# Splitting weight pieces with two GpSimd-issued transfers and one ScalarE operation in a hybrid decoder block

## The chip, the cores and the metric

The kernel runs on one core of one Trainium2 chip. The metric is the device time of one execution in microseconds. Below, PE is the matrix engine, DVE is VectorE, ACT is ScalarE, POOL is GpSimd and SP is SyncE; SP, ACT and POOL can issue DMA transfers.

## The reference

For 512 tokens of 1024 channels, one decoder layer is computed:

```
u = rmsnorm(h);  P = u @ W_in            # combined projection, 8280 columns
A = gated delta rule over q, k, v (causal conv, chunks, 8 heads), gated norm
B = sparse attention: indexer picks top 128 causal keys per query, 8 heads
m = sigmoid(gate_A) * A + sigmoid(gate_B) * B
h = h + m @ W_out
h = h + (silu(conv(hn @ W_up_gate)) * conv(hn @ W_up_val)) @ W_down
out = rmsnorm(h)
```

Everything is float32.

## The kernel before

The weights lie in DRAM as 139 **pieces** of 128 rows by 1024 values (512 KB each), in the order in which they are used (`_pack_weights`). A product with float32 accuracy is made of three passes in the format float32r (L201 to L203): each operand is held as a high part (the value rounded to float32r) and a low part (the rest), and low by high, high by low and high by high are summed in PSUM. The weights' parts are the tiles `whi` and `wlo`; the activations' parts are `xgh`/`xgl`, `uTh`/`uTl`, `mix`, `hTh`/`hTl` and `act`. A piece feeds 24 matmuls of 512 columns or 48 of 256.

`load` (L183) brings a piece from DRAM into the tile `raw` by a transfer on SP. `piece` (L191) then makes the parts: ACT rounds `raw` into `whi` (L193), and POOL or DVE subtracts, `wlo = raw - whi` (L194). The callers choose the engine: `token_major` and `channel_major` give the pieces of the mixers to POOL, except that the second piece of each pair in the second half of the delta rule goes to DVE (L494, L508, L546); the output projection (L832), the up projection from its third group on (L904) and the down projection (L950) give theirs to DVE. `raw`, `whi` and `wlo` have three buffers each, so up to three loaded and three split pieces wait ahead of PE. The first three pieces are split by halves in `split` (L229), which the change leaves alone.

The order of the work on each engine is found by the scheduler of the tile framework, which places instructions by a simulated timeline; a few pairs are ordered by hand (`after`). Around the pieces stand: the start (x, the value projection, the norm; L234 to L277), the decay and the indexer (L337 to L450, DVE chains `gd` and `iq`/`iqf`), the gated delta rule in two halves (`gdn_half`, L467), each with an inverse of 32x32 blocks on DVE (L571 to L579: tiles `wi`, `tw`), the top-128 search (L676 to L680), the attention (L696 to L729), the gates (L735 to L802), the output projection (L831), the up projection (L903) and the down projection (L943). POOL also makes `uTl` (L417), the masks `ge` (L522), scaled queries `qT` (L540) and the gate products (L764) between the pieces.

The lines that the change touches most:

```
def piece(lo_engine):
    raw, hi, lo = load()
    A.copy(hi, raw)
    lo_engine.tensor_sub(lo, raw, hi.bitcast(F))
    return hi, lo
```

Of the kernel before, what the change touches and what calls it, by code (L numbers as in the profile page):

```python
# [9 lines left out]
F = mybir.dt.float32  # L10
R = mybir.dt.float32r
I32 = mybir.dt.int32
AF = mybir.ActivationFunctionType
OP = mybir.AluOpType
# [4 lines left out]
D = 1024  # L19
# [22 lines left out]
def _in_chunks():  # L42
    """The projection's columns in the order in which the kernel takes them."""
    t = []
    t.append(("dv", [_DV, _DV + 128]))
    t.append(("small", None))
    t += [("iq", [_IQ + 256 * j, _IQ + 256 * j + 128]) for j in range(2)]
    gdn = [[("gdn", [_QKV + 1024 * part + 512 * hh + 256 * j + 128 * i for i in range(2)])
            for part in (1, 0, 2) for j in range(2)] for hh in range(2)]
    dsa = [("dk", [_DKV, _DKV + 128])]  # L50
    dsa += [("dq", [_DQ + 256 * j, _DQ + 256 * j + 128]) for j in range(4)]
    t += gdn[0] + dsa + gdn[1]
    off = {"z": _Z, "ga": _GA, "gb": _GB}
    t += [(k, [off[k] + 256 * j, off[k] + 256 * j + 128]) for k, j in _GATES]
    return t


def _pack_weights(w_in, w_out, w_up, w_down):
    """All weights as pieces of [128 rows, 1024 values], in the order of their use."""
    out = []  # L60

    def chunk(w, starts):
        c = np.concatenate([w[:, s:s + 128] for s in starts], axis=1)
        c = c.reshape(2, 4, 128, 256).transpose(0, 2, 1, 3).reshape(2, 128, 1024)
        out.extend([c[0], c[1]])

    for kind, starts in _in_chunks():
        if kind == "small":
            c = np.zeros((D, 128), w_in.dtype)
            c[:, 0:64] = w_in[:, _IK:_IK + 64]  # L70
            c[:, 64:80] = w_in[:, _A:_A + 16]
            c[:, 80:88] = w_in[:, _IW:_IW + 8]
            out.append(c.reshape(8, 128, 128).transpose(1, 0, 2).reshape(128, 1024))
        else:
            chunk(w_in, starts)
    for j in range(4):
        chunk(w_out, [256 * j, 256 * j + 128])
    for f in range(NF):
        chunk(w_up, [128 * f, FF + 128 * f])
    for half in range(2):  # L80
        c = w_down[:, 512 * half:512 * half + 512].reshape(NF // 2, 2, 128, 512)
        out.extend(c.transpose(0, 2, 1, 3).reshape(NF // 2, 128, 1024))
    return np.ascontiguousarray(np.stack(out))
# [3 lines left out]
def hybrid_block(ctx: ExitStack, tc: tile.TileContext, x: bass.AP, xc: bass.AP, wp: bass.AP,  # L87
# [22 lines left out]

# [1 line left out]
    ident = const.tile([128, 128], F, name="ident")  # L112
# [14 lines left out]
    def after(ins, before):  # L127
        """Keeps the order of two instructions of one engine."""
        tc.add_manual_dep(ins.ins, before.ins.name,
                          mybir.DependencyInfo(mybir.DependencyClass.NoSync, mybir.DependencyReason.DATA),  # L130
                          reason="order")
        return ins

    def rsqrt(y, v, tmp, it):
        """y = 1/sqrt(v) by Newton's steps from the bits' estimate."""
        V.tensor_scalar(it, v.bitcast(I32), -0.5, 1597463007.0, op0=OP.mult, op1=OP.add)
        cur = it.bitcast(F)
        for _ in range(3):
            V.scalar_tensor_tensor(tmp, cur, -0.5, cur, op0=OP.mult, op1=OP.mult)
            V.tensor_mul(tmp, tmp, v)  # L140
            V.scalar_tensor_tensor(y, tmp, 1.5, cur, op0=OP.add, op1=OP.mult)
            cur = y
# [13 lines left out]
    def part_of(ss, name, bufs, part=(eps, neps), eng=V):  # L156
        """ss/D + part, and -1/2 of it, of one value per partition."""
        p = const.tile([128, 2], F, name=name, bufs=bufs)
# [4 lines left out]
    def rms_of(ss, part=(eps, neps), out=None):  # L163
        """1/sqrt(ss/D + part) of one value per partition; a Newton step makes up for the table."""
        w = const.tile([128, 5], F, name="rms", bufs=4)
# [9 lines left out]
    def load_sqrt(after):  # L175
        """Brings in the square root's table once the value `after` is there."""
        A.activation(warm, after, AF.Sqrt, scale=0.0, bias=ones[:, 0:1])

# [1 line left out]
    pipe = ctx.enter_context(tc.tile_pool(name="pipe", bufs=1))  # L180
    pos = [0]

    def load():  # L183
        raw = pipe.tile([128, 1024], F, name="raw", bufs=3)
        nc.sync.dma_start(raw, wp[pos[0]])
        pos[0] += 1
        hi = pipe.tile([128, 1024], R, name="whi", bufs=3)
        lo = pipe.tile([128, 1024], R, name="wlo", bufs=3)
        return raw, hi, lo

    def piece(lo_engine):  # L191
        raw, hi, lo = load()
        A.copy(hi, raw)  # L193
        lo_engine.tensor_sub(lo, raw, hi.bitcast(F))  # L194
        return hi, lo

    def passes(o, lhs, rhs, first, last, shared=False):
        """o += lhs^T rhs with both operands in two parts. In a shared bank only the bank's first
        product carries the start, which clears the marks of the whole bank."""
        (lh, ll), (rh, rl) = lhs, rhs  # L200
# [9 lines left out]

# [1 line left out]
    wz = psum.tile([128, 512], F, name="wz", tag="rec", bufs=2)  # L212
# [77 lines left out]
    def token_major(eng):  # L290
        """One 256-column chunk: two banks, each with two token blocks [128, 2, 256]."""
        pcs = [piece(eng), piece(eng)]
# [19 lines left out]

# [1 line left out]
    PR = tc.alloc_tile_pool(name="PR", bufs=1, side="right", reuse_waits="tile")  # L314
# [6 lines left out]

# [1 line left out]
    dv = PR.tile([128, NT, 256], F, name="dv", tag="k4", bufs=2)  # L323
# [3 lines left out]

# [1 line left out]
    smT = PR.tile([128, 512], F, name="smT", tag="y", bufs=2)  # L329
# [6 lines left out]

# [1 line left out]
    def red(o, i, op=OP.add):  # L338
# [23 lines left out]

# [1 line left out]
    def sc8(name):  # L364
# [46 lines left out]

# [1 line left out]
    for k in range(KT):  # L413
# [3 lines left out]
        (V, P)[k % 2].tensor_sub(uTl[:, k], uv, uTh[:, k].bitcast(F))  # L417
# [1 line left out]
    iq = []  # L419
# [13 lines left out]

# [1 line left out]
    score = {}  # L435
# [15 lines left out]

# [1 line left out]
    def conv_silu(p, ti, dst=None):  # L453
# [13 lines left out]
    def gdn_half(hh):  # L467
# [23 lines left out]

        # keys
        for j in range(2):
# [11 lines left out]
        V.tensor_mul(kd, rk, kde[:, :, hs])  # L505
        # queries
        for j in range(2):
# [7 lines left out]

        # decayed products of keys with keys and queries
        for c in range(NT):
# [25 lines left out]

        # values
        for j in range(2):
# [8 lines left out]

        # inverses of the diagonal 32x32 blocks, one block per partition
        bl = dram.tile([64, 1024], F, name="bl%d" % hh)
# [23 lines left out]

        # merge the blocks: 32 -> 64 -> 128
        UT = PL.tile([128, 16, 64], F, name="UT", tag="g4", bufs=2)
# [32 lines left out]

        # the recurrence over chunks
        St = PL.tile([128, HH, 128], F, name="St", tag="St")
# [32 lines left out]

        # gated norm of the heads, up to the gate
        so = sc("so")
# [16 lines left out]

# [1 line left out]
    V.memset(mask[:, 0:128], 0.0)  # L671
# [9 lines left out]

# [1 line left out]
    dk = PR.tile([128, 2, 512], F, name="dk", tag="k4", bufs=2)  # L683
# [49 lines left out]

# [1 line left out]
    h_t = FL.tile([128, NT, D], F, name="h")  # L735
# [67 lines left out]

# [1 line left out]
    hTh = const.tile([128, KT, S], R, name="hTh", tag="uTh")  # L805
# [9 lines left out]
    def channels(tb, hn, order=None):  # L815
        """hn of one token block to channel-major parts; `order`: the product that goes before."""
        for q in range(2):
# [60 lines left out]

# [1 line left out]
    act = []  # L880
# [42 lines left out]

# [1 line left out]
    gf = FR.tile([128, D], F, name="gf")  # L925
# [102 lines left out]
```

## Time and profile before

| | us |
|---|---|
| three runs, median (lowest to highest) | 972.58 (971.25 to 973.08) |
| the profiled execution, first to last instruction (span) | 966.1 |
| busy: PE / DVE / ACT / POOL | 928.7 / 626.6 / 440.9 / 203.2 |
| splitting: ACT rounding, 136 pieces | 142.6 |
| splitting: subtraction on POOL, 60 pieces | 146.1 |
| splitting: subtraction on DVE, 76 pieces | 94.3 |

The profile gives the profiled execution's span alone; the median of the runs is 6.5 us above it, and that difference stands for what lies around the span. Busy time is time in which an engine has an instruction under way; a matmul's end is modelled, so a busy PE need not be at its best pace.

### The profile page before, as it was taken

Reading aid. Unit: us, or ns where it says so; the run is one execution under the profiler, and the core shown is the slowest. Engines: PE = TensorE matmul, PEld = TensorE weight load, DVE = VectorE, ACT = ScalarE, POOL = GpSimd, SP = SyncE. Lnnn points to the kernel's source line nnn. Section 1 sums busy time; section 2 is a strip of 40 time slices with the busy share of each in tenths; the row PEclk is TensorE's granted clock in tenths of the full one; section 3 lists DMA queues with packets and bytes.
Section 4 is the critical chain, followed back from the end, with each engine's and each line's share of the span. In section 5 each row is a group of like instructions: output and inputs, shape, how many; then the busy total and the mean of one; then the engine's idle time right before and its main releaser. Section 6 shows DMA issues by size and latency. Waiting matters only on the chain.

```text
span 966.1 us, 14640 instructions
## 1 busy us (share of the span) xinstructions
PE 928.7 (96%) x5671; PEld 801.9 (83%) x5671; DVE 626.6 (65%) x1262; ACT 440.9 (46%) x938; POOL 203.2 (21%) x116
## 2 busy tenths in 40 slices
PE   8979999998899899899999999999999999999997
PEld 8858887876787798799999999888888888888886
DVE  5897999997638969866663546655555655522424
ACT  7446674422367773245543436443434443422213
POOL 3734244412011263211244032000000000000201
PEclk9989999999999999999999999999999999999999
DMA  8222222323310131311323222332223223232222
GB/s 326 88 88 88 89 83 71 112 83 89 99 34 26 62 89 66 99 51 50 135 85 104 83 89 88 108 97 99 88 87 98 99 89 107 88 108 90 88 66 87
DMA packets 35381, 88.76 MB, mean 92 GB/s; under 512 B 11472, under 2 KB 12784, under 8 KB 35312
## 3 DMA queue, kind: packets, MB, share of 16 engines
q1 hardware_dynamic: 24048, 82.05, 25.7%
q10 hardware_dynamic: 11264, 5.79, 2.4%
q8 instruction: 44, 0.72, 0.3%
q14 instruction: 25, 0.20, 0.1%
HBM read 84.66 MB, written 3.16 MB: 91 GB/s over the span
## 4 chain that ended last, share of the span: by engine, by line
PE 72%; DVE 20%; ACT 3%; DMA 2%; issue 1%; ACTq 0%; POOL 0%; SPq 0%; DVEq 0%
PE acc L201 18%; PE acc L203 18%; PE acc L202 18%; DVE y L458 3%; PE d L202 3%; PE d L203 3%; PE d L201 3%; DVE tw L574 2%; DVE wi L576 2%; PE lg L700 1%; DVE mask L679 1%; PE lg L718 1%; DVE top L678 1%; DMA MT<-bl 1%; DVE mask L448 1%
## 5 line engine op out<-in xcount | busy, mean ns | idle before, releaser
L193 ACT CAST whi<-raw 128x1024 fp32r<-128x1024 f32 x136 | 142.6, 1049 | 175.7 <-PE acc L203 76.8
L194 POOL TENSOR_TENSOR wlo<-raw,whi 128x1024 fp32r<-128x1024 f32 x60 | 146.1, 2436 | 309.7 <-ACT whi L193 275.4
L194 DVE TENSOR_TENSOR wlo<-raw,whi 128x1024 fp32r<-128x1024 f32 x76 | 94.3, 1241 | 149.7 <-ACT whi L193 149.6
L202 PE MATMUL acc<-hTh,wlo 128*128 128x512 f32 (+1 forms) x368 | 141.8, 385 | 0.0
L201 PE MATMUL acc<-hTl,whi 128*128 128x512 f32 (+1 forms) x368 | 141.1, 386 | 0.3 <-DVE hTl L827 0.3
L203 PE MATMUL acc<-hTh,whi 128*128 128x512 f32 (+1 forms) x368 | 140.8, 385 | 0.0
L201 PE MATMUL acc<-uTl,whi 128*128 128x512 f32 x272 | 110.0, 405 | 8.7 <-DVE iqf L423 5.5
L202 PE MATMUL acc<-uTh,wlo 128*128 128x512 f32 x272 | 109.7, 403 | 4.8 <-DVE wlo L194 4.8
L201 PE MATMUL acc<-wlo,uTh 128*128 128x256 f32 x384 | 111.2, 290 | 0.0
L202 PE MATMUL acc<-whi,uTl 128*128 128x256 f32 x384 | 110.9, 289 | 0.0
L203 PE MATMUL acc<-whi,uTh 128*128 128x256 f32 x384 | 109.8, 286 | 0.0
L203 PE MATMUL acc<-uTh,whi 128*128 128x512 f32 x272 | 109.1, 402 | 0.0
L886 DVE SCALAR_TENSOR_TENSOR fy<-acc,ch,fy 128x511 f32<-128x511 f32 x88 | 65.8, 749 | 28.8 <-ACT fy L884 27.0
L968 POOL TENSOR_TENSOR h<-h,gf 128x512 f32<-128x512 f32 (+1 forms) x8 | 10.6, 1344 | 346.9 <-ACT sq L964 346.9
L201 PEld LDWEIGHTS acc<-hTl,whi 128*128 128x128 f32 x368 | 69.2, 188 | 15.6 <-DVE hTl L827 0.5
L202 PEld LDWEIGHTS acc<-hTh,wlo 128*128 128x128 f32 x368 | 69.2, 188 | 15.2
L203 PEld LDWEIGHTS acc<-hTh,whi 128*128 128x128 f32 x368 | 69.2, 188 | 15.2
L202 PEld LDWEIGHTS acc<-whi,uTl 128*128 128x128 f32 x384 | 72.6, 189 | 1.5 <-issue 1.2
L203 PEld LDWEIGHTS acc<-whi,uTh 128*128 128x128 f32 x384 | 72.6, 189 | 1.4 <-issue 1.0
L201 PEld LDWEIGHTS acc<-wlo,uTh 128*128 128x128 f32 x384 | 72.5, 189 | 0.9 <-issue 0.2
L201 PEld LDWEIGHTS acc<-uTl,whi 128*128 128x128 f32 x272 | 51.8, 191 | 21.1 <-DVE iqf L423 5.9
L202 PEld LDWEIGHTS acc<-uTh,wlo 128*128 128x128 f32 x272 | 51.7, 190 | 16.4 <-DVE wlo L194 5.7
(311 smaller groups left out, 1931.5 us busy)
## 6 DMA issues: line engine op xcount, KB each, us to landing
raw<-in_wp_dram SPq DMA_DIRECT2D x139, 512.0 KB, 3.4
xT<-in_xc_dram SPq DMA_DIRECT2D x8, 256.0 KB, 5.6
xt<-in_x_dram SPq DMA_DIRECT2D x4, 512.0 KB, 7.8
ge<-gdr ACTq DMA_DIRECT2D x8, 256.0 KB, 3.5
h<-in_x_dram SPq DMA_DIRECT2D x4, 512.0 KB, 6.9
out_dram<-h SPq DMA_DIRECT2D x8, 256.0 KB, 2.1
gbias<-in_rows_dram ACTq DMA_DIRECT2D x8, 128.0 KB, 3.0
bl<-MT ACTq DMA_DIRECT2D x8, 64.0 KB, 2.2
```

What stands on the lines that cost most here:

```text
L193: A.copy(hi, raw)
L194: lo_engine.tensor_sub(lo, raw, hi.bitcast(F))
L201: a = T.matmul(o, lh, rl, start=first, stop=False, skip_group_check=shared)
L202: T.matmul(o, ll, rh, start=False, stop=False, skip_group_check=shared)
L203: return a, T.matmul(o, lh, rh, start=False, stop=last, skip_group_check=shared)
L448: V.scalar_tensor_tensor(score[b], p, w, score[b], op0=OP.mult, op1=OP.add)
L458: V.scalar_tensor_tensor(y[:, s:], p[:, :512 - s], cw[:, ti, 3 - s:4 - s], y[:, s:], op0=OP.mult, op1=OP.add)
L574: V.tensor_mul(w, wi[:, 0:j, j:j + 1].to_broadcast([64, j, m]), nn[:, j:j + 1, j + 1:].to_broadcast([64, j, m]))
L576: V.tensor_sub(wi[:, 0:j, j + 1:], wi[:, 0:j, j + 1:], w)
L678: V.max(top, score[b])
L886: V.scalar_tensor_tensor(y[:, s:], p[:, :512 - s], fw[:, ti, 2 - s:3 - s], y[:, s:], op0=OP.mult, op1=OP.add)
L968: P.tensor_mul(hv, hv, gf[:, 512 * half + c.start:512 * half + c.stop])
```

## The change

`piece` no longer loads a raw copy. POOL issues a transfer from DRAM straight into the float32r tile `whi`, which converts on the way; ACT writes `wlo = -whi`; POOL issues a second transfer of the same piece from DRAM that adds into `wlo`. So each piece is read from DRAM twice, and both transfers stand in POOL's queue. `whi` and `wlo` get four buffers in place of three; `raw` is only used by the first three pieces and moves to the pool of the start. The engine argument of the callers is ignored. Comments and docstrings are dropped, so lines from 175 on move by five.

```diff
+    def parts():
+        return tuple(pipe.tile([128, 1024], R, name=n, bufs=4) for n in ("whi", "wlo"))
+
     def load():
-        raw = pipe.tile([128, 1024], F, name="raw", bufs=3)
+        raw = sr.tile([128, 1024], F, name="raw", bufs=3)
         nc.sync.dma_start(raw, wp[pos[0]])
         pos[0] += 1
-        hi = pipe.tile([128, 1024], R, name="whi", bufs=3)
-        lo = pipe.tile([128, 1024], R, name="wlo", bufs=3)
-        return raw, hi, lo
-
-    def piece(lo_engine):
-        raw, hi, lo = load()
-        A.copy(hi, raw)
-        lo_engine.tensor_sub(lo, raw, hi.bitcast(F))
+        return (raw, *parts())
+
+    def piece(lo_engine=None):
+        hi, lo = parts()
+        w = wp[pos[0]]
+        pos[0] += 1
+        P.dma_start(hi, w)
+        A.activation(lo, hi.bitcast(F), AF.Copy, scale=-1.0)
+        P.dma_start(lo, w, accum_op=OP.add)
         return hi, lo
```

Two places of POOL's queue show how the instructions move; L197 is the converting transfer and L199 the adding one, and the number behind a tile's name tells instances apart.

In the up projection POOL has nothing to do in the kernel before (from the third group on). In the changed kernel its queue repeats this pattern, a pair of pieces at a time:

```order
L197 DMA whi_7163<-in_wp_dram 128x1024 [waits DMASW0_49,PE_49]
L197 DMA whi_7168<-in_wp_dram 128x1024 [waits DMASW1_49,PE_49]
L199 DMA wlo_7164<-in_wp_dram 128x1024 [waits DMASW2_49,Activation_49]
L199 DMA wlo_7169<-in_wp_dram 128x1024 [waits DMASW3_49,Activation_49]
L197 DMA whi_7236<-in_wp_dram 128x1024 [waits DMASW4_49,PE_49]
L197 DMA whi_7241<-in_wp_dram 128x1024 [waits DMASW5_49,PE_49]
```

A load waits for PE to let go of a buffer, and the adding transfer of a pair's first piece stands behind the load of its second.

In the second half of the delta rule, where the gates' pieces begin, POOL's queue before is this:

```order
L194 TENSOR_TENSOR wlo_4242<-raw_4239,whi_4241 128x1024 [waits DVE_49,DMAHW4_49,PE_49,Activation_49]
L540 TENSOR_TENSOR qT_2384<-qT_2384,ge_2814 128x4x128 [waits DVE_49,PE_49]
L194 TENSOR_TENSOR wlo_4248<-raw_4245,whi_4247 128x1024 [waits DMAHW5_49,Activation_49]
L522 AFFINE_SELECT ge_2880<-ge_2880 128x512 [waits DMAHW0_49,DVE_49,Pool_49]
L540 TENSOR_TENSOR qT_2384<-qT_2384,ge_2847 128x4x128 [waits PE_49]
```

And in the changed kernel:

```order
L197 DMA whi_4317<-in_wp_dram 128x1024 [waits DMASW4_49,PE_49]
L545 TENSOR_TENSOR qT_2358<-qT_2358,ge_2780 128x4x128 [waits DVE_49,PE_49]
L199 DMA wlo_4318<-in_wp_dram 128x1024 [waits DMASW6_49,DMASW5_49,Activation_49]
L527 AFFINE_SELECT ge_2846<-ge_2846 128x512 [waits DMAHW4_49,DVE_49,Pool_49]
L769 TENSOR_TENSOR at_812<-at_812,tz_4191 128x2x256 [waits DVE_49]
L545 TENSOR_TENSOR qT_2358<-qT_2358,ge_2813 128x4x128 [waits PE_49]
L197 DMA whi_4322<-in_wp_dram 128x1024 [waits PE_49]
```

The load of a piece, which was on SP's queue, now stands on POOL's behind the mixers' own instructions. The order of PE's matmuls is nearly the same as before.

## Rows read from the trace of the kernel before

**Rows 1.** The page: busy time of each engine, and the chain's shares.

```profile
PE 928.7 (96%) x5671; PEld 801.9 (83%) x5671; DVE 626.6 (65%) x1262; ACT 440.9 (46%) x938; POOL 203.2 (21%) x116
...
PE 72%; DVE 20%; ACT 3%; DMA 2%; issue 1%; ACTq 0%; POOL 0%; SPq 0%; DVEq 0%
```

**Rows 2.** Busy time by stretch: delta rule's first half, up projection.

```profile
core 0: us, PE busy (x) PEld busy (x) DVE busy (x) ACT busy (x) POOL busy (x), PEclk, DMA share, GB/s
65.00:165.00 100.00, 98.79 (x480) 81.26 (x479) 92.26 (x215) 60.28 (x162) 39.93 (x22) 1.00 0.28 89
...
605.00:660.00 55.00, 55.00 (x237) 44.34 (x236) 32.24 (x40) 23.73 (x31) 0.00 (x0) 1.00 0.32 100
```

**Rows 3.** The timeline of PE, idle time before an instruction in brackets.

```profile
58.77 0.79 PE L201 MATMUL acc<-uTl,whi 128*128 128x512 f32 x1 [5.47 <-DVE iqf L423]
...
213.22 0.50 PE L202 MATMUL acc<-uTh,wlo 128*128 128x512 f32 x1 [2.23 <-DVE wlo L194]
...
224.48 0.50 PE L202 MATMUL acc<-uTh,wlo 128*128 128x512 f32 x1 [2.60 <-DVE wlo L194]
...
244.78 0.47 PE L201 MATMUL acc<-uTl,whi 128*128 128x512 f32 x1 [2.44 <-DVE y L458]
...
406.03 0.24 PE L591 MATMUL m<-UT,MT 32*32 32x32 f32 x2 [1.15 <-DVE UT L585]
409.36 1.19 PE L591 MATMUL m<-UT,MT 32*32 32x32 f32 x62 [1.18 <-DVE UT L585]
```

**Rows 4.** Groups of instructions by line: the splitting of 136 pieces.

```profile
L194 POOL TENSOR_TENSOR wlo<-raw,whi 128x1024 fp32r<-128x1024 f32 x60 | 146.1, 2436 | 309.7 <-ACT whi L193 275.4 <-issue 18.7 <-DVE h L861 8.6
L193 ACT CAST whi<-raw 128x1024 fp32r<-128x1024 f32 x136 | 142.6, 1049 | 175.7 <-PE acc L203 76.8 <-PE d L203 71.6 <-issue 10.1
...
L194 DVE TENSOR_TENSOR wlo<-raw,whi 128x1024 fp32r<-128x1024 f32 x76 | 94.3, 1241 | 149.7 <-ACT whi L193 149.6
```

**Rows 5.** The timelines of POOL and DVE at subtractions on POOL.

```profile
44.92 2.76 POOL L194 TENSOR_TENSOR wlo<-raw,whi 128x1024 fp32r<-128x1024 f32 x1 [1.55 <-ACT whi L193]
...
45.45 2.77 DVE L428 TENSOR_TENSOR iq<-iqf,iq 64x512 fp32r<-64x512 f32 x1
...
50.15 0.69 DVE L428 TENSOR_TENSOR iq<-iqf,iq 64x512 fp32r<-64x512 f32 x1
...
206.81 2.40 POOL L194 TENSOR_TENSOR wlo<-raw,whi 128x1024 fp32r<-128x1024 f32 x1 [8.80 <-ACT whi L193]
...
206.57 0.38 DVE L574 TENSOR_TENSOR tw<-wi,nn 64x220 f32<-64x220 f32 x1
206.98 2.47 DVE L576 TENSOR_TENSOR wi<-wi,tw 64x220 f32<-64x220 f32 x1
...
371.28 2.46 DVE L574 TENSOR_TENSOR tw<-wi,nn 64x210 f32<-64x210 f32 x1
...
393.69 2.45 DVE L576 TENSOR_TENSOR wi<-wi,tw 64x168 f32<-64x168 f32 x1
```

**Rows 6.** Transfers: issues on SP and ACT, a piece's time to landing, SP's queue.

```profile
L185 SPq DMA_DIRECT2D raw<-in_wp_dram x139: 327/328/432, 1.7 to 928.2; - x139
...
DMA to landing us min/median/max: 3.3/3.4/10.3
...
q1 hardware_dynamic: 24048, 82.05, 25.7%
```

**Rows 7.** ACT: an operation of the new one's kind and shape (ns min/median/max).

```profile
L270 ACT ACTIVATE xn<-xt x4: 1043/1044/1062, 14.9 to 19.1; 128x1024 f32<-128x1024 f32 x4
```

**Rows 8.** Who waited for whom: POOL's waits in the mixers (us, times, longest).

```profile
POOL at L764 <- DVE tz L762: 14.2, 6, 3.9
...
POOL qT L540 <- PE kk L533: 12.4, 3, 6.3
...
POOL ge L522 <- DMA ge<-gdr: 11.1, 3, 7.7
...
POOL ge L522 <- PE kk L533: 4.6, 1, 4.6
```

## The prediction

> **What bounds the kernel now.** I read the busy times first, then the chain of waits, then the stretches, and last the idle time on PE's own timeline. PE is busy for 928.7 of 966.1 us, and the chain that ended last lies on PE for 72% and on DVE for 20% [rows 1]. In the up projection 237 matmuls take 55.00 us with PE never idle at the full granted clock [rows 2], so one piece (24 matmuls of 512 columns) takes PE 24 x 0.232 = 5.57 us. There DVE is busy for 32.24 of 55 us and POOL not at all: an engine that splits weights sets no time there, and nothing taken from it gains any. The 8 + 44 + 22 = 74 pieces of the last three products run in this manner.
>
> What can be gained is PE's idle time, 966.1 - 928.7 = 37.4 us, and it lies almost all in the first 450 us. The larger waits are for DVE [rows 3]: 5.47 us for `iqf`, 2.23 and 2.60 for `wlo`, 2.44 for the convolution, 1.15 and 1.18 for the inverse. DVE is nearly full there, 92.26 of 100 us [rows 2]. And it is slowed: where a subtraction runs on POOL, a two-input DVE operation takes as long as that subtraction. `iq` takes 2.77 us beside one and 0.69 us without; `wi` takes 2.47 us where the `tw` of the same size just before took 0.38 [rows 5].
>
> **What the change removes and adds.** *Removed:* 60 subtractions on POOL (146.1 us), 76 on DVE (94.3 us) [rows 4] and 136 loads on SP. *ACT* does one operation of the same shape as before: 1.049 us for the rounding [rows 4], 1.044 for an ACTIVATE of 128x1024 [rows 7]; it costs nothing new. *POOL* issues 272 transfers. The trace shows none from POOL. The nearest row is an issue on SP, 0.328 us [rows 6], and the upper bound I take is POOL's own subtraction, 2.44 us; four issues per pair then take 1.3 to 9.8 us of the 11.1 us that PE spends on a pair, so POOL's time suffices at either end. I take a value near the lower end, as an issue moves no data through the engine. The Trainium skill ("DMA: Bandwidth & Descriptors", Specifications) gives about 1 us to first byte for a transfer from GpSimd and 0.6 from SP or ACT; no run here shows it, and by it the sum would be the same.
>
> *The DMA engines.* SP's queue moved 82.05 MB in 25.7% of 966.1 us [rows 6], so a piece (0.524 MB) costs 248.3 x 0.524 / 82.05 = 1.59 us of all sixteen. The converting transfer I take at the same 1.59 us, since it moves the same bytes. The adding transfer must read its destination too; the trace shows none. Its bounds are 1.59 us (as a plain one) and three times that, 4.8 us (two reads and a write one after the other); I take twice, 3.2 us, because reading and writing overlap in a plain transfer as well. Together 4.8 us per piece against PE's 5.57: the engines are 86% full in the last three products, and still hidden.
>
> *The lead time.* With four buffers a load may start when PE has left the piece four before it, 3 x 5.57 = 16.7 us ahead of need. Then come two issues, the landing (3.4 us as for a raw piece [rows 6]), ACT's 1.05 us, and the adding transfer's landing (3.4 + 1.6 = 5.0 us, an estimate from the doubled reading): 9.5 us plus issues of 0.7 to 4.9 us, 10.2 to 14.4 us. The first piece of a pair queues its addition behind the second's load, which waits 5.57 us longer: 5.57 + two issues + 5.0, 11.2 to 15.5 us. Both end ahead of 16.7, so in the last three products the change is worth 0.
>
> *The mixers, against the profiled span of 966.1 us.*
> - `wlo` on DVE behind the first inverse: the two waits of 2.23 + 2.60 us go, **-4.8 us** (bounds -4.8 to 0, if the new `wlo` is as late).
> - The start: the 5.47 us wait for `iqf` stands at the end of a DVE chain that meets several POOL subtractions, each about 2 us [rows 5]. They go; four `uTl` on POOL stay. **-5.5 us** (bounds -5.5 to +3, the latter if the first pieces, whose loads now queue behind those `uTl`, come late).
> - The inverses: three operations in the first and four in the second (from 371.28 to 393.69) are held some 2 us each [rows 5], so each chain ends 6 to 8 us sooner. PE waits only 2.44, 1.15 and 1.18 us there [rows 3]; half of that, **-2.5 us** (bounds -4.8 to 0), because the next thing late is the delta rule's own transfers.
> - POOL's queue: loads and additions now stand behind instructions that wait 14.2 + 12.4 + 11.1 + 4.6 = 42.3 us in all [rows 8]. Behind the waiting POOL instruction queue the next pieces, and PE waits for those; the cover is three ready pieces, 16.7 us, and the longest single wait is 7.7. **+4 us** (bounds 0 to +21, half of the 42.3).
>
> Sum: -4.8 - 5.5 - 2.5 + 4 = -8.8, a span of 957.3 us. The three runs' median lies 6.5 us above the profiled span, which the change does not touch: **963.8 us, given as 964**. With its bounds this case reaches from 956 to 970.
>
> **Rivals.**
> - *The transfers become the bound* (slower). It decides where the two transfers together pass 5.57 us per piece, that is where the addition costs more than 2.5 plain transfers. For it: each piece is read twice, added into memory, and no row shows such a transfer; against: at twice a plain one it fits. At three plain ones a piece needs 6.4 us and the 74 pieces of the last products lose 74 x 0.8 = 61 us: 964 + 61 = 1025 us. If conversion also costs double, 8.0 us per piece: 74 x 2.4 = 180, 1144 us.
> - *POOL's queue starves PE in the mixers* (slower). Half of the 42.3 us of waits [rows 8] turns into PE's idle time: 964 - 4 + 21 = 981 us. For it: a held load now delays the whole chain of load, ACT and addition, where SP's loads ran ahead of everything; against: ready pieces cover 16.7 us. DVE operations could hold POOL's issues as POOL's subtractions hold DVE now; at 0.7 us for each of some 40 issues while DVE is full, 28 us, it ends in the same place. The Trainium skill ("SBUF — State Buffer", Who interferes with whom, and the box on the trap of DVE blocking DMA) says that a transfer issued from GpSimd waits while DVE runs an operation that takes both ports, which speaks against this change; the DVE rows here are mostly two-input operations, of which the page says that they hold up only reads, so I leave it in this rival.
> - *Gains and losses cancel*, 972 us: PE's waits for DVE turn into waits for the adding transfer at the same places.
>
> **How the numbers follow.** The forecast 0.50; transfers as the bound 0.22; starved by POOL's queue 0.19; cancelled 0.09. A measurement of this kernel can tell about 0.2%, 1.9 us, from no change. So faster 0.50, same 0.09, slower 0.41. The range reaches from the forecast's lower end, 956, over the starved case and the lighter half of the transfer-bound case to 1035; left out are about 0.06 below and 0.12 above. The forecast's own range is 956 to 970.
>
> **What the profile would show.** Right: in the up projection PE still takes 55 us for some 237 matmuls and waits for no `wlo`; the DMA share there rises from 0.32 to about 0.86; no `wi` or `iq` takes over 2 us on DVE; PE's waits for `iqf` and `wlo` are gone before 250 us; POOL's issues are under 1 us. Wrong: PE waiting for `whi` or `wlo` through the up and down projections (then the DMA share or the landing of L199 tells whether width or lead time failed), or such waits only between 60 and 450 us behind POOL's `ge`, `qT` or `at` (POOL's queue).

## The result and the profile after

The changed kernel takes **1015.43 us** (median of 4 runs, 1011.49 to 1017.83) against 971.91 us of the kernel before in the same series: a ratio of 1.0456, interval 1.0431 to 1.0482. The prediction was 964.0 us with an interval of 956 to 1035 and 0.50 for faster: the direction is wrong. The profiled execution has a span of 1009.8 us.

The profile's page of the changed kernel: busy times, the chain's shares, the queue of POOL's transfers, three groups (busy, mean ns, idle before), and the transfers' landing (median us).

```profile
PE 946.0 (94%) x5671; PEld 812.7 (80%) x5671; DVE 479.9 (48%) x1186; ACT 438.0 (43%) x938; POOL 249.5 (25%) x328
...
q0 software_dynamic: 39168, 142.62, 63.1%
...
PE 54%; issue 17%; DMA 16%; POOL 6%; ACT 4%; DVE 2%; ACTq 1%; SPq 0%; POOLq 0%; DVEq 0%
...
L198 ACT ACTIVATE wlo<-whi 128x1024 fp32r<-128x1024 f32 x136 | 143.9, 1059 | 376.0 <-DMA whi<-in_wp_dram 326.9
L199 POOL DMA_DIRECT2D wlo<-in_wp_dram x136 | 120.5, 886 | 459.6 <-ACT wlo L198 403.6
L197 POOL DMA_DIRECT2D whi<-in_wp_dram x136 | 91.6, 684 | 215.2 <-PE acc L208 193.3
...
whi<-in_wp_dram POOLq DMA_DIRECT2D x136, 512.0 KB, 6.0
wlo<-in_wp_dram POOLq DMA_DIRECT2D x136, 512.0 KB, 5.6
```

Beside [rows 1] and [rows 4]: DVE lost 147 us of work, as meant, and left the chain (2% in place of 20%). In its place stand issues and transfers, 33% together. POOL waits 403.6 us for ACT, and ACT 326.9 us for landings: the two engines hand one long wait to each other. PE's idle time grew from 37.4 to 63.8 us (1009.8 - 946.0).

PE's timeline at eight of its waits, the idle time before a matmul in brackets:

```profile
31.57 0.80 PE L207 MATMUL acc<-xgh,wlo 128*128 128x512 f32 x1 [3.14 <-DMA wlo<-in_wp_dram]
...
197.78 0.50 PE L207 MATMUL acc<-uTh,wlo 128*128 128x512 f32 x1 [1.11 <-DMA wlo<-in_wp_dram]
206.03 0.50 PE L207 MATMUL acc<-uTh,wlo 128*128 128x512 f32 x1 [2.10 <-DMA wlo<-in_wp_dram]
214.06 0.50 PE L207 MATMUL acc<-uTh,wlo 128*128 128x512 f32 x1 [2.17 <-DMA wlo<-in_wp_dram]
223.40 0.50 PE L207 MATMUL acc<-uTh,wlo 128*128 128x512 f32 x1 [1.92 <-DMA wlo<-in_wp_dram]
...
292.23 0.33 PE L719 MATMUL pT<-ident,pe 128*128 128x128 f32 x1 [4.15 <-ACT pe L711]
...
609.21 0.39 PE L206 MATMUL acc<-wlo,mix 128*128 128x256 f32 x1 [3.73 <-DMA wlo<-in_wp_dram]
...
941.03 0.50 PE L206 MATMUL d<-wlo,act 128*128 128x512 f32 x1 [2.24 <-DMA wlo<-in_wp_dram]
```

The waits of [rows 3] for `iqf` and for DVE's `wlo` are gone; waits for the adding transfer, every 8 to 9 us around 210 us, have come where the latter stood. Waits cost more than their own length. Around 210 us the granted clock is 0.91, where it was 0.96 before; and in the 5 us of the longest wait, which ended at 292.23, it falls from 1.00 to 0.82 and is 0.84 in the 5 us behind, where PE is never idle. Busy time by stretch (PE, PEld, DVE, ACT, POOL, then clock, DMA share, GB/s): the first line is the kernel before, the others the changed one.

```profile
193.00:233.00 40.00, 34.79 (x142) 26.98 (x141) 38.44 (x85) 10.15 (x13) 7.32 (x3) 0.96 0.22 81
...
196.00:236.00 40.00, 32.20 (x119) 23.98 (x118) 26.62 (x76) 8.33 (x11) 7.70 (x11) 0.91 0.67 163
...
285.00:290.00 5.00, 3.07 (x24) 2.74 (x22) 3.17 (x11) 1.32 (x2) 0.00 (x0) 1.00 0.63 171
290.00:295.00 5.00, 2.77 (x15) 2.47 (x16) 0.33 (x2) 4.54 (x19) 0.86 (x1) 0.82 0.66 104
295.00:300.00 5.00, 5.00 (x38) 4.70 (x37) 2.66 (x8) 2.25 (x8) 0.00 (x0) 0.84 0.00 1
```

Over the span the mean clock is 0.978 against 0.990. Its shortfall is (1 - 0.978) x 1009.8 = 22.2 us against 9.7; by this estimate the clock accounts for 12.5 of the 17.3 us by which PE's busy time grew.

**Where the time went, by stage.** The matmuls that read a weight piece (4266 of the 5671) run in nearly the same order in these kernels, so the start of the same one in that order can be read in two traces. The table gives that start minus the one in the kernel before, for the matmul that starts there at the time above (the last column is the difference of the spans); it is also used below. Where the attention's matmuls move between the pieces, between 163 and 405 us, neighbouring matmuls differ by some us, so there only large differences count.

| at (us, before) | 82 | 203 | 245 | 275 | 325 | 365 | 487 | 527 | 588 | 647 | 848 | span |
|---|---|---|---|---|---|---|---|---|---|---|---|---|
| changed kernel | -2.8 | +6.5 | +5.3 | +11.2 | +14.4 | +21.1 | +16.8 | +20.8 | +34.3 | +33.9 | +33.9 | +43.7 |
| five buffers (`whi5`) | -3.4 | -4.4 | -15.3 | -15.3 | -16.9 | -15.0 | -10.9 | -10.3 | -10.2 | -11.0 | -11.0 | -10.9 |
| `add_mixers` | +2.4 | +2.2 | -7.5 | -7.5 | -8.0 | -10.5 | -16.5 | -15.1 | -14.9 | -15.5 | -15.5 | -15.4 |
| `all_dve` | -11.3 | -11.7 | -23.8 | -27.4 | +12.1 | +5.1 | -15.5 | -13.8 | -13.3 | -14.2 | -14.2 | -14.1 |
| `hybrid` | -11.6 | -8.6 | -21.2 | -19.1 | -13.8 | -16.4 | -25.9 | -25.3 | -25.2 | -26.0 | -26.0 | -25.9 |

The changed kernel loses nothing in the up projection (from 590 to 836 us), where the transfer engines are busiest. It loses in the mixers (6.5 us by 203 us, 21.1 by 365), just before and in W_out (from 20.8 at 527 to 34.3 at 588) and in the down projection (from 33.9 to 43.7). A 55 us stretch of the up projection, beside the one of [rows 2]:

```profile
639.00:694.00 55.00, 55.00 (x238) 44.30 (x237) 20.39 (x28) 23.04 (x30) 14.36 (x20) 1.00 0.83 185
```

**The loop in POOL's queue.** The place around 210 us shows what is late. POOL's timeline, then ACT's negations:

```profile
200.39 0.87 POOL L199 DMA_DIRECT2D wlo<-in_wp_dram  x1 [6.67 <-ACT wlo L198]
200.95 0.88 POOL L197 DMA_DIRECT2D whi<-in_wp_dram  x1
208.64 0.86 POOL L199 DMA_DIRECT2D wlo<-in_wp_dram  x1 [6.82 <-ACT wlo L198]
209.19 1.42 POOL L197 DMA_DIRECT2D whi<-in_wp_dram  x2
217.21 0.89 POOL L199 DMA_DIRECT2D wlo<-in_wp_dram  x1 [6.61 <-ACT wlo L198]
```

```profile
207.29 1.06 ACT L198 ACTIVATE wlo<-whi 128x1024 fp32r<-128x1024 f32 x1 [6.72 <-DMA whi<-in_wp_dram]
215.86 1.06 ACT L198 ACTIVATE wlo<-whi 128x1024 fp32r<-128x1024 f32 x1 [7.04 <-DMA whi<-in_wp_dram]
```

The load issued at 200.95 has landed at 207.29, ACT negates it until 208.35, POOL issues its addition at 208.64, and only then, at 209.19, the next loads. That is a loop of 8.25 us for a piece that PE uses up in 5.57. No buffer is waited for: the next load simply stands behind the addition. In the order in which POOL issued the transfers, 85 of the 136 additions have no later piece's load ahead of them: 44 of the 62 ahead of W_out, 5 of 8 in W_out, 13 of 22 in the down projection, and 23 of 44 in the up projection, where two loads go out together and the second of two additions has none.

### The profile page after: what moved, and what is told of

It reads as the page before. It is cut to its first block, busy times and chain, and to the rows that moved or that the text cites. A ratio compares the mean times of both kernels' runs of the same rounds, so it can differ in the third digit from the quotient of the medians.

```text
span 1009.8 us, 14668 instructions
## 1 busy us (share of the span) xinstructions
PE 946.0 (94%) x5671; PEld 812.7 (80%) x5671; DVE 479.9 (48%) x1186; ACT 438.0 (43%) x938; POOL 249.5 (25%) x328
## 4 chain that ended last, share of the span: by engine, by line
PE 54%; issue 17%; DMA 16%; POOL 6%; ACT 4%; DVE 2%; ACTq 1%; SPq 0%; POOLq 0%; DVEq 0%
PE acc L207 14%; PE acc L208 14%; PE acc L206 14%; DMA whi<-in_wp_dram 9%; DMA wlo<-in_wp_dram 2%; POOL wlo L199 2%; DMA ge<-gdr 2%; POOL whi L197 2%; ACT wlo L198 2%; PE d L206 1%; PE lg L723 1%; PE d L208 1%; PE d L207 1%; DMA xt<-in_x_dram 1%; PE lg L705 1%
## 5 line engine op out<-in xcount | busy, mean ns | idle before, releaser
L198 ACT ACTIVATE wlo<-whi 128x1024 fp32r<-128x1024 f32 x136 | 143.9, 1059 | 376.0 <-DMA whi<-in_wp_dram 326.9
L199 POOL DMA_DIRECT2D wlo<-in_wp_dram x136 | 120.5, 886 | 459.6 <-ACT wlo L198 403.6
L197 POOL DMA_DIRECT2D whi<-in_wp_dram x136 | 91.6, 684 | 215.2 <-PE acc L208 193.3
L206 PE MATMUL acc<-hTl,whi 128*128 128x512 f32 (+1 forms) x368 | 138.9, 386 | 0.4 <-DVE hTl L832 0.4
L207 PE MATMUL acc<-uTh,wlo 128*128 128x512 f32 x272 | 111.6, 410 | 10.1 <-DMA wlo<-in_wp_dram 10.1
L208 PE MATMUL acc<-whi,uTh 128*128 128x256 f32 x384 | 112.8, 294 | 0.0
L207 PEld LDWEIGHTS acc<-uTh,wlo 128*128 128x128 f32 x272 | 52.6, 193 | 23.8 <-DMA wlo<-in_wp_dram 12.6
L463 DVE SCALAR_TENSOR_TENSOR y<-acc,cw,y 128x511 f32<-128x511 f32 (+2 forms) x72 | 53.1, 742 | 29.3 <-ACT y L461 28.9
```

Source lines behind the costliest of these rows:

```text
L197: P.dma_start(hi, w)
L198: A.activation(lo, hi.bitcast(F), AF.Copy, scale=-1.0)
L199: P.dma_start(lo, w, accum_op=OP.add)
L206: a = T.matmul(o, lh, rl, start=first, stop=False, skip_group_check=shared)
L207: T.matmul(o, ll, rh, start=False, stop=False, skip_group_check=shared)
L208: return a, T.matmul(o, lh, rh, start=False, stop=last, skip_group_check=shared)
```

## The experiments

My theory after this reading was the loop, that is, the order in POOL's queue together with the landing; rivals were the width of the transfer engines, the number of buffers, and ACT's queue.

**Where it is lost.** `old_late`: the pieces of the last three products as before.

```diff
-        pcs = [piece(V), piece(V)]
+        pcs = [old_piece(V), old_piece(V)]
```

> The mixers' and gates' 62 pieces keep the new split; the 74 pieces of W_out, the up and the down projection go back to the old one (load by SP, rounding on ACT, subtraction on DVE). Theory (waits for the new pieces, stage by stage): by the same matmuls of both timelines the changed kernel loses 25 us before W_out, 9 in W_out, 0 in the up projection and 10 in the down projection, so this one gets 19 of 43.5 us back: 996 us, with PE's idle time after 590 us as in the kernel before. Rival (the loss is one of width: the transfers set a slower pace wherever they run): the up projection is the longest such stretch and should then give back most, 975 us or less.

991.46 us (ratio to before 1.0227, interval 1.0198 to 1.0257): 24 us come back, a little more than the theory's 19, and 22 remain in the mixers and gates. Taking the transfers out of the up projection gave nothing back there (24.0 us late at 607 us and at 848 us alike); the transfer engines' width as the pace is out.

**The fifth buffer and the order.** `whi5`:

```diff
-        return tuple(pipe.tile([128, 1024], R, name=n, bufs=4) for n in ("whi", "wlo"))
+        return tuple(pipe.tile([128, 1024], R, name=n, bufs=b) for n, b in (("whi", 5), ("wlo", 4)))
```

> One more buffer of whi (five instead of four; wlo keeps four, no more fits). Theory (lead time): the converting transfer can start one piece, some 5.6 us, sooner, so it has landed when ACT and POOL come to the piece; ACT's waits for it (326.9 us) fall below 150, PE's waits for the adding transfer (24.9 us) below 10, and the time to about 985 us. Rival (width): the same bytes through the same engines, a buffer more changes nothing: 1008 us or more, and the waits only move.

**955.37 us** (0.9852, 0.9803 to 0.9901): 60 us less than the changed kernel, and faster than the kernel before. More than the theory gave: PE's waits for the adding transfer fell from 24.9 to 3.3 us, those for `pe` and `pT` from 14.6 to 3.7. First PE's waits for the adding transfer in the changed kernel and the one left here (us, times, longest), then POOL's waits here, which show why:

```profile
PE acc L207 <- DMA wlo<-in_wp_dram: 13.3, 7, 3.1
...
PE acc L206 <- DMA wlo<-in_wp_dram: 5.9, 3, 3.7
PE d L206 <- DMA wlo<-in_wp_dram: 5.7, 4, 2.2
```

```profile
PE acc L207 <- DMA wlo<-in_wp_dram: 3.3, 1, 3.3
...
POOL whi L197 <- PE acc L208: 416.8, 96, 30.0
POOL wlo L199 <- ACT wlo L198: 111.6, 112, 4.8
```

Now POOL waits above all for PE to let go of a buffer, and for ACT 111.6 us in place of 403.6. But the edit did two things: the scheduler, with a fifth buffer, also put the load of the next piece ahead of every addition but the last. `order4` and `hold5` separate them, by a fixed order of the two issues (`after` keeps it), with four buffers and with five. In `order4` a list `ahead` holds the loads that are issued already; its addition comes behind the last of them. In `hold5` a load comes behind the addition of the piece before.

```diff
+        while len(ahead) < 2 and pos[0] < wp.shape[0]:
+            head()
...
+        add = P.dma_start(lo, w, accum_op=OP.add)
+        if ahead:
+            after(add, ahead[-1][2])
```

```diff
+        d = P.dma_start(hi, w)
+        if prev:
+            after(d, prev[-1])
...
+        prev.append(P.dma_start(lo, w, accum_op=OP.add))
```

> Four buffers as in the changed kernel; only the order in POOL's queue is fixed: the converting transfer of piece k+1 always stands ahead of the adding transfer of piece k (in the changed kernel that is so for every second piece at best, and for none in long stretches of the mixers). Theory (queue order): where the next load stands behind the addition, a piece costs a loop of issue, landing, ACT and issue, 0.7 + 6.0 + 1.06 + 0.9 = 8.7 us against PE's 5.57; with two landings in flight the loop is halved, so PE's waits for wlo go as with five buffers: 955 to 970 us. Rival (buffers): the fifth buffer was what helped; with four the load waits for PE's release and the addition now waits behind it: 1000 us or more.

> Five buffers of whi, but the converting transfer of piece k+1 is held behind the adding transfer of piece k in POOL's queue, always. Theory (queue order): the loop of one piece, at the least 0.55 + 3.7 + 1.06 + 0.9 = 6.2 us and up to 8.7, exceeds PE's 5.57 everywhere, the up projection too, and the spare buffer stays empty: over 1015 us, up to 1090. Rival (buffers): the release by PE sets the start of a load, so five buffers give 955 to 965 us in either order.

`order4`: 980.26 us (1.0102, 1.0079 to 1.0126), between the two expectations; `hold5`: **1231.15 us** (1.2698, 1.2639 to 1.2756), as the theory has it, and beyond the 1090 us of its upper end. The order alone, at four buffers, is worth 35 of the 60 us, and at five its absence costs 276: with every load held behind an addition the spare buffer is never used. A 55 us stretch of `hold5`'s up projection:

```profile
700.00:755.00 55.00, 44.94 (x170) 34.43 (x168) 16.02 (x22) 17.75 (x24) 10.04 (x14) 0.91 0.58 127
```

170 matmuls make 55 / 170 x 24 = 7.8 us per piece, inside the 6.2 to 8.7 of the theory, while the engines are less busy than in the changed kernel (0.58 against 0.83). The rival on buffers is right in part: with the good order the fifth buffer gives the other 25 us. Why four are too few then was not tried. By its waits POOL's loads wait 473.0 us for PE in `order4`, with the additions behind them; PE's waits for the adding transfer are 13.5 us there, between the 24.9 of the changed kernel and the 3.3 of `whi5`; and it loses 5.9 us between the matmuls at 588 and 848 us, where the changed kernel loses none.

`order5x2`: `order4` with five buffers and two loads ahead of each addition.

```diff
-        while len(ahead) < 2 and pos[0] < wp.shape[0]:
+        while len(ahead) < 3 and pos[0] < wp.shape[0]:
```

> Five buffers of whi, and two converting transfers ahead of each adding one. Theory (queue order): one load ahead is enough for the loop; the second takes ACT's waits for landings (123 us with five buffers) to nearly nothing, but the addition now waits for the release of one more buffer: 950 to 965 us. Rival (ACT's queue matters by itself): with ACT never held by a landing, PE's last waits for pe, pT and oB go as well: below 950.

959.02 us (0.9891, 0.9863 to 0.9918): no better than one ahead. ACT's waits for landings fell from 123.0 to 92.9 us only, so the second load's effect on ACT stays mostly untested.

**The price of adding.** `no_accum`: the second transfer overwrites.

```diff
-        P.dma_start(lo, w, accum_op=OP.add)
+        P.dma_start(lo, w)
```

> The second transfer writes w over wlo instead of adding it (the low parts are wrong by that: wlo holds the rounded weight, not the remainder). All waits and the order stay. It prices the accumulation: Theory A (adding takes twice a plain transfer of all sixteen engines, 3.1 us against 1.6): the dynamic queue's share of 63% falls to about 42%, and the landings with it, and the time to 985 us. Rival B (the conversion costs the engines as much as the addition, 2.3 us each): the share stays near 63% and the time near 1010.

943.03 us (0.9719, 0.9696 to 0.9742), below both expectations. From its page:

```profile
q0 software_dynamic: 39168, 142.62, 50.5%
...
whi<-in_wp_dram POOLq DMA_DIRECT2D x136, 512.0 KB, 4.0
wlo<-in_wp_dram POOLq DMA_DIRECT2D x136, 512.0 KB, 3.9
```

A converting transfer takes 0.505 x 940.4 / 272 = 1.75 us of all sixteen engines; if it costs the same in the changed kernel, the adding one takes (0.631 x 1009.8 - 136 x 1.75) / 136 = 2.93 us. The dearer half is the addition, though less than twice (the share fell to 50%, not 42). This kernel has the very order of POOL's queue that the changed one has, and does not suffer: its loop is about 0.54 + 4.0 + 1.06 + 0.3 = 5.9 us, near PE's 5.57. So it takes both, the order and the landing that the addition in front of it stretches from 4.0 to 6.0 us. The trace of the changed kernel shows the same: of the 86 loads that follow an addition in POOL's queue, the 66 issued within 2 us of it landed in a median of 6.3 us, the 20 issued later in 4.0.

**Who negates.** `neg_pool` and `neg_dve` put the negation on POOL and on DVE (`V` for `P` in the line below).

```diff
-        A.activation(lo, hi.bitcast(F), AF.Copy, scale=-1.0)
+        P.tensor_scalar(lo, hi.bitcast(F), -1.0, None, op0=OP.mult)
```

> The negation moves from ACT to POOL, ahead of the adding transfer in the same queue; nothing of the weights is left on ACT. Theory (ACT's queue is held by negations that wait for a landing, with the attention's pe and pT behind them): PE's waits for pe and pT (14.6 us) go, and with the clock that they cost some 20 us: about 995 us, if POOL's operation takes no more than 1.5 us. Rival (lead time alone): the chain of a piece gets longer by what POOL's operation takes over ACT's 1.06 us, and POOL's operations hold DVE's as the subtractions did before: 1015 to 1040 us.

> The changed kernel with the negation on DVE in place of ACT; the order in POOL's queue is nearly the same (no load ahead of the addition in long stretches of the mixers, every second piece in the up projection). Theory (queue order): the loop of landing, negation and issue keeps its length, so the time stays between 1000 and 1030 us. Rival (ACT's queue, held by negations that wait for a landing, cost the changed kernel its time by PE's waits for pe and pT, 14.6 us and the clock after them): those waits go, 985 us or less.

`neg_pool`: 1113.5 us (1.1484, 1.1446 to 1.1522), above what both theories gave. POOL's operation takes 2.80 us, not 1.5, and it stands in the loop:

```profile
L198 POOL TENSOR_SCALAR wlo<-whi 128x1024 fp32r<-128x1024 f32 x136 | 380.8, 2801 | 284.5 <-DMA whi<-in_wp_dram 284.1
```

`neg_dve`: 1034.65 us (1.0663, 1.0636 to 1.069), a little above the theory's 1000 to 1030. With ACT free of the pieces, PE's waits for `pe` and `pT` halved (14.6 to 6.9 us), but those for the adding transfer rose (24.9 to 43.0 us):

```profile
PE acc L207 <- DMA wlo<-in_wp_dram: 17.0, 7, 3.8
PE d L206 <- DMA wlo<-in_wp_dram: 14.5, 6, 6.7
PE acc L206 <- DMA wlo<-in_wp_dram: 11.5, 6, 4.5
...
PE lg L723 <- ACT pT L721: 3.7, 2, 3.0
...
PE pT L719 <- ACT pe L711: 3.2, 5, 1.2
```

The run does not give the 985 us that ACT's queue as the cause would, but alone it does not clear ACT, since the negation now waits in DVE's queue (POOL waits 385.7 us for it). `whi5` does: the negation is still on ACT there, and the waits for `pe` and `pT` fell to 3.7 us. The attention behind a held negation is how part of the loop reaches PE, not where it comes from.

**What there was to save.** `add_for_pool` starts from the kernel before and replaces only POOL's 60 subtractions; loads stay on SP. `add_mixers` leaves the first four pieces of the up projection to DVE. `all_dve` has no new transfer: it moves POOL's 60 subtractions to DVE. First the edit of the first two (`load` also gives `w`, the piece in DRAM), then that of `all_dve`.

```diff
         A.copy(hi, raw)
-        lo_engine.tensor_sub(lo, raw, hi.bitcast(F))
+        if lo_engine is P:
+            A.activation(lo, hi.bitcast(F), AF.Copy, scale=-1.0)
+            P.dma_start(lo, w, accum_op=OP.add)
+        else:
+            lo_engine.tensor_sub(lo, raw, hi.bitcast(F))
```

```diff
-        lo_engine.tensor_sub(lo, raw, hi.bitcast(F))
+        V.tensor_sub(lo, raw, hi.bitcast(F))
```

> The kernel before, with loads by SP, rounding on ACT and DVE's subtractions as they were; only POOL's 60 subtractions become a negation on ACT and an adding transfer. Theory (the collisions of POOL's subtractions with DVE's operations are what the change can save): their removal is worth the 5 to 9 us that the prediction gave the mixers, and loads by SP don't stand in POOL's queue: 960 to 965 us. Rival (the adding transfer's landing is as late as the subtraction was, and 60 more operations of 1.05 us on ACT hold the attention): 970 to 985 us.

> The kernel in which only POOL's subtractions became adding transfers (956.8 us), with the first two of the up projection's groups given to DVE's subtraction, so that 56 pieces, all ahead of W_out, are added by a transfer. Theory (the adding transfer pays where DVE is full and costs where PE's pace is fixed): the 2.09 us wait at the start of the up projection and the clock after it go, 3 to 4 us: 953 us. Rival (it was the landing of any piece there, raw ones too): no change, 957 us.

> The kernel before with all 136 subtractions on DVE, no new transfer at all. Theory (what the change can save is that POOL's subtractions hold DVE's operations): the collisions go, but 60 x 1.24 = 74 us of work come to a DVE that is 92% busy in the mixers, so that PE waits for it there: 975 to 1000 us. Rival (the subtractions cost a held DVE more than 1.24 us each, so that DVE ends no later than before): 955 to 968 us, and then the adding transfer is not needed for the gain.

956.83 us (0.9867, 0.9825 to 0.991), 952.28 us (0.9809, 0.9789 to 0.983) and 954.0 us (0.9829, 0.9809 to 0.9849). The first is better than its theory (960 to 965), the second as its theory gave it (953). The third went against my theory: DVE does 60 x 1.24 = 74 us more, and PE ends 14.1 us sooner. It is behind only around 325 to 405 us, and there in part because PE works in another order: the attention's `pT` of 284 us is made 42 us earlier. From the page of `all_dve` and its groups:

```profile
PE 932.6 (98%) x5671; PEld 807.5 (85%) x5671; DVE 629.5 (66%) x1322; ACT 441.6 (46%) x938; POOL 63.4 (7%) x56
```

```profile
L194 DVE TENSOR_TENSOR wlo<-raw,whi 128x1024 fp32r<-128x1024 f32 x136 | 167.7, 1234 | 163.6 <-ACT whi L193 163.3
```

DVE is busy for 629.5 us, 2.9 more than before [rows 1]. Its records overlap, so a group's time can't be taken off the total; by the records without the subtractions, DVE's other 1186 operations cover 538.2 us in the kernel before and 475.5 us here. The 60 subtractions on POOL had cost DVE 63 us, 1.0 us each, most of what doing them takes. In the changed kernel, where only the first three pieces are still subtracted, they cover 479.9 us. A gain like those of `whi5` and `add_for_pool`, 14 us each, is thus to be had without any adding transfer: here it is 17 us.

`hybrid` takes DVE's subtraction early and in two of the gates, the adding transfer for 28 pieces between; of its edits to `add_mixers`, the first and the last:

```diff
-        for t, p in enumerate(channel_major(P, xg)):
+        for t, p in enumerate(channel_major(V, xg, V)):
...
-        for t2, p in enumerate(token_major(P)):
+        for t2, p in enumerate(token_major(V)):
```

> Subtractions on DVE in the first 160 us (indexer queries, keys and queries of the first half) and in the gates ga and gb, adding transfers for 28 pieces between (values, sparse attention's projections, first pieces of the second half, gate z). By the same matmuls, the kernel with all subtractions on DVE led the kernel before by 12.4 us at 163 us and then lost that lead by 203 us, while the one with 56 adding transfers ran level up to 203 us and gained 19 us from there to 487 us. Theory (each is right where the other loses: DVE has room early, and is late in the inverses): both gains join, 938 to 948 us. Rival (the lead of the early part is used up by the next late thing, the delta rule's own chain): 950 to 954 us, as each alone.

**943.66 us** (0.9703, 0.9678 to 0.9729), the fastest of all kernels here that do the whole computation with nothing left out. The total is as the theory gave it, and the stages bear its reason out in the main: of the early lead (11.6 us at 82) 8.6 us are left at 203, another 12.6 are gained up to 245, and the lead is 25.9 at 487. One figure of the expectation is not so: by the table `all_dve` has not lost its lead at 203 us, but still has 11.7 us there.

## Why the prediction was wrong

- **DVE and POOL's subtractions: right.** `iq` takes at most 0.69 us in the changed kernel, the `wi` of the inverse's steps at most 0.40 (2.47 in [rows 5]) and `tw` at most 1.34. In the kernel before, five steps of the first inverse took 1.7 to 2.5 us, not three. The three mixer terms were -12.8 us; with five buffers, where the loop is gone, the kernel is 15.3 us ahead at 245 us and 10.9 at the end. In the changed kernel itself they are not seen by themselves, since the loop's loss lies over them. The 5.47 us wait for `iqf` went; a 3.14 us wait at 31.57 gave part of it back.
- **ACT, and POOL's issues: right.** 1.06 us against 1.05 [rows 4, 7]; 0.68 and 0.89 us per issue on average. The Trainium skill ("SBUF — State Buffer", Who interferes with whom) has DVE operations that take both ports hold such issues; no such hold is seen here, where between 65 and 165 us, with DVE 81% busy, 14 loads were issued in 0.53 to 0.88 us each. The same section says that a DVE operation with two inputs in SBUF contends with a POOL instruction that reads there; [rows 5] and the 63 us of `all_dve` agree.
- **The price on the transfer engines: right.** 1.75 + 2.93 = 4.7 us per piece, predicted 1.59 + 3.2 = 4.8; a share of 0.83, predicted 0.86; 55.00 us for 238 matmuls in the up projection. The rival of transfers as the bound did not occur.
- **The step that failed is the lead time**: "With four buffers a load may start when PE has left the piece four before it, 3 x 5.57 = 16.7 us ahead of need". A load starts when its place in POOL's queue comes up, and in 85 of 136 cases that is behind the addition of the piece before, which waits for ACT, which waits for a landing. I had taken the pairwise order of the up projection, where it held (0 lost), for all products; 34 us are lost ahead of the up projection, where it mostly did not hold: 25 before W_out (25.1 at 540 us) and 9 in it (34.3 at 588). Another 10 are lost in the down projection; for the last three products the prediction had 0. The landing was a second error in the same sum: the load took 6.0 us, not 3.4, since 66 of the 136 loads were issued within 2 us of an addition ahead of them. The adding transfer's 5.6 us was near the 5.0. These two do not explain all: with the order set right, four buffers still give 980 us (`order4`), 16 more than the forecast, so 16.7 us ahead of need was too much to count on in that order too; why stays open.
- **POOL's queue, +4 us (0 to +21): the right resource, the wrong term.** I counted POOL's waits for the mixers' own work [rows 8]. With five buffers those still stand (`ge` 30.0 us, `qT` 15.3) and the time is 955 us: they were covered. The loop of the pieces' own issues, not in the sum, costs 35 us by the order alone (`order4`) and 60 us over the kernel with five buffers. The rival that put 981 us on POOL's queue had the place and not the mechanism: what holds a load is the addition of the piece before, not the mixers' work.
- **Sums, and luck.** The terms' own bounds add up to 957.5 to 996.6 us, not to the 956 to 970 given; and of PE's idle time 30.5 of the 37.4 us, not almost all, lie before 450 us. The measured time lies between 956 and 1035 only because that interval was drawn wide for two slower cases, neither of which came about as described: that is luck.

## What to carry to other kernels

When loads and the work that depends on them are issued from one in-order queue, write down the loop from a load's issue to the next load's issue, landing included; if a dependent issue stands between, that loop can set the pace while buffers are free and the transfer engines have room. Read the order at every stage and not at one, and put the next load ahead of the dependent issue, with a buffer for it. Before an engine's work is moved into transfers to spare another, try it on the spared engine itself: 60 subtractions on POOL cost DVE 63 us, doing them 74.

## What the runs showed of the hardware beyond expectation

- A transfer that adds took 2.93 us of all sixteen engines for 512 KB, one that only converts 1.75, both worked out from the queue's share (`no_accum`). Its issue on POOL took 0.89 us on average against 0.54 when the same line did not add.
- A negation of 128x1024 values took 2.80 us on POOL, 1.06 on ACT and 0.71 on DVE.
- The mean granted clock was 0.990 in the kernel before, 0.978 in the changed one, 0.931 in `hold5` and 0.998 in `hybrid`, with PE idle for 37.4, 63.8, 205.5 and 19.7 us. The sum of PE's waits does not settle it: in `all_dve`, with 19.4 us, it was 0.985.
